# Four-layer hybrid trunk in fp32 on one core: the first block pairs built together, and the dense layers' matrix products kept in source order

## Chip, cores and metric

One core of one Trainium2 chip. The metric is the device time of one execution in microseconds; for the kernel before it is the median of three runs. Further readings come from one profiled execution.

## The reference, cut to what matters

```python
def rmsnorm(x, g):
    y = x * lax.rsqrt(jnp.mean(x * x, axis=-1, keepdims=True) + RMS_EPS)
    return y * g

def short_conv_mixer(h, w_in, conv_w, w_out):
    b_gate, c_gate, z = jnp.split(h @ w_in, 3, axis=-1)
    conv = causal_depthwise_conv(c_gate * z, conv_w)      # width 3
    return (b_gate * conv) @ w_out

def swiglu_ffn(h, w_gate, w_up, w_down):
    return (jax.nn.silu(h @ w_gate) * (h @ w_up)) @ w_down

def reference(x, ...):                                    # x: 512 tokens x 1024
    for i in range(4):                                    # conv, gating, retention, conv
        x = x + mixer[i % 3](rmsnorm(x, norm_mix_g[i]))
        x = x + swiglu_ffn(rmsnorm(x, norm_ffn_g[i]))     # hidden width 2816
    return rmsnorm(x, final_norm_g)
```

The gating and the retention mixer are not touched by the change and are left out here. All is float32.

## The kernel before, in words

**Layout.** `x` lies transposed in SBUF, features on partitions: four tiles `x0` to `x3` of 128 x 1024, each a pair of 128-feature blocks by 512 tokens. The RMS norm is not applied to `x` ahead of a layer: products are made with `x` times its gain, and their results are multiplied by the token's scale afterwards (`normed`), so the scale may come late.

**Three products for one.** The products on TensorE (PE) take operands of type `F32R`. Each float32 operand is split into a high part (a cast on ScalarE, ACT) and a low part (source minus high part, on VectorE, DVE) by `split` (L174); a product is then high x high, high x low and low x high into one PSUM accumulator. `product` (L181 to L195) issues these matmuls at L193; of its last term it issues all three at the end, so that a late last operand holds back only those.

**Seven-part form.** In the conv mixers and in the FFNs a pair of 128-column blocks of weights, against pairs of input blocks and two halves of the tokens (256 each, `H`), is multiplied by a scheme with seven products instead of eight (`columns7`, L211). It uses sums of the inputs (`th`, `tl`, made by `operand_sums`, L409 to L429, from `x` times gain) and sums of the weights (L136 to L139 and the split of the sums). Three accumulators, `c1`, `c5` and `c2` (names ending in 1, 5 and 2 in the program), take the seven parts, 12 matmuls of 256 columns each. `c1` is used several times: between its parts ACT or DVE reads it, at L240, L245 and, with a sign flip, L256:

```python
        part(c1, 3, xt, 1, False)
        with self.tc.high_priority(SOON):
            nc.vector.scalar_tensor_tensor(y[:, 2 * H : 3 * H], c1, -1.0, m5, ALU.mult, ALU.subtract)
        def end():
            part(c1, 2, xt, 3, False)
            nc.scalar.mul(y[:, 3 * H :], c1, -1.0)
            self.held.append(partial(then, y))
        self.late = end
```

The last part, `end`, and what follows from the result (`then`) are put off: `finish` (L284) issues them in the next form, behind that form's first two parts. The plain form with eight products, `columns4` (L262), has two accumulators of 512 columns, 24 matmuls each, and calls `finish` at its start. The first block pair of each layer (`m == 0`) uses the plain form, as the input sums are not needed there.

**Layers.** `conv` loops over four block pairs `m`; for each it builds the three projections `pc`, `pz`, `pb`, and DVE and ACT work out the gated convolution (`first`, `second`, `third`, L575 to L595), which leaves the operands `yh`, `yl`. `ffn` loops over eleven block pairs of the hidden width in four parts: `pg`, `pu`, then SiLU and product leave `hidh`, `hidl`; the down projection `out` of a part is issued by `leave` behind the first `pg` of the next part. `leave` (L433 to L464) adds `out` to `x` (L457), and in its final pass makes the next layer's operands (`operand`, L406 and L407, or L403, L420 and the splits) and the squares (L318 to L322). `end` does this for the last layer, in token halves.

**Scale.** In the first `then` of a layer, `scale_in_psum` sums the squares to a column per 128 tokens by small matmuls (L366, named `scale`), ACT takes a root (L333) and DVE four small steps (L334 to L337); a diagonal (L383) and one more matmul (L384, named `rps`) spread the scale over the partitions. `end` does it through `last_scale`.

**What sets the order.** The program is written in source order, and a scheduler then orders each engine's instructions by a model of its own; products may pass each other. `keep_in_program_order` ties an instruction to the one before it on its engine in source order; before the change only the scale's small matmuls (L368) and the last norm's products have it. The mixed layers (gating, retention) run in `mixed()`, the convs and the FFNs in `dense()`; only inside `dense()` is the pool `self.w7` set, and it holds the weights of the seven-part products.

**Weights and the start.** `plan` and `plan7` list the weight chunks in the order of use; `weights` fetches up to three chunks ahead of the one in use, each half chunk through one of four `raw` buffers of 512 KB by a DMA on SyncE's queue (L127 for the plain form), and splits it. At the start, `run` loads `x0` in two halves, then `x1` to `x3` whole (512 KB each); between them `first_weights` (L166) loads the first plain `pc` chunk in four pieces of 256 KB. The `pz` and `pb` chunks of the first pair follow as ordinary chunks of two 512 KB transfers. `begun` is the last operand made of the loaded `x`; the input sums and the squares of the first layer are issued behind it, in the middle of the first round of `conv`'s loop.

Of the kernel before, what the change touches and what calls it, by code (L numbers as in the profile page):

```python
# [17 lines left out]
P = 128  # L18
# [24 lines left out]
class Kernel:  # L43
# [72 lines left out]
    def prepare7(self, i):  # L116


        nc = self.nc
        src, _, plain = self.chunks[i]  # L120
        out = [[] for _ in range(8)]
        for half in range(2):
            if plain:
                raw = self.raw.tile([P, 4, NB // 4, P], F32, tag="raw", name=f"raw{i}{half}")
                h, l = (self.wp.tile([P, 4, NB // 4, P], F32R, tag=part, name=f"w{part}{i}{half}") for part in "hl")
                if i:
                    nc.sync.dma_start(raw, src[half])  # L127
                    self.split(raw, h, l)
                else:
                    self.first.append((raw, src[half], h, l))  # L130
                for j in range(4):
                    out[j] += [(h[:, j, k], l[:, j, k]) for k in range(NB // 4)]
                continue
            raw = self.raw.tile([P, 4, NB // 4, P], F32, tag="raw", name=f"raw{i}{half}")
            sums = self.sums.tile([P, 4, NB // 4, P], F32, tag="sums", name=f"sums{i}{half}")
            nc.sync.dma_start(raw, src[half])  # L136
            nc.vector.tensor_add(sums[:, :2], raw[:, 3:].broadcast_to([P, 2, NB // 4, P]), raw[:, :3:2])  # L137
            nc.vector.tensor_add(sums[:, 2], sums[:, 1], raw[:, 0])
            nc.vector.tensor_add(sums[:, 3], sums[:, 2], raw[:, 1])  # L139
            for x, n, first, pool in ((raw, 3, 0, self.w7), (sums, 4, 3, self.wp)):  # L140
                h, l = (pool.tile([P, n, NB // 4, P], F32R, tag=part, name=f"w{part}{i}{half}{n}") for part in "hl")
                self.split(x[:, :n], h, l)
# [20 lines left out]
        self.next += 1  # L163
        return self.ready.pop(i)

    def first_weights(self, i, j):  # L166

        raw, src, h, l = (t[:, j : j + 2] for t in self.first[i])
        self.nc.sync.dma_start(raw, src)
        self.split(raw, h, l)  # L170

    def split(self, src, h, l):

# [8 lines left out]
    def product(self, ps, terms, first=True, last=True, more=False):  # L182
# [7 lines left out]
        lh, ll, rh, rl = terms[-1]  # L190
        seq += [(lh, rh), (lh, rl), (ll, rh)]
        for i, (x, y) in enumerate(seq):
            nc.tensor.matmul(  # L193
                ps, x, y, start=first and i == 0, stop=last and i == len(seq) - 1, skip_group_check=more
            )  # L195

    def columns(self, name, acts):

# [66 lines left out]
    def columns4(self, name, then, hold=False, kept=True):  # L265
# [6 lines left out]
        for even, odd in ((0, 1), (3, 2)):  # L272
# [3 lines left out]
                terms += [(*w[even][k], h[:, :T], l[:, :T]), (*w[odd][k], h[:, T:], l[:, T:])]  # L276
            self.product(ps, terms)
            out.append(ps)
        y = self.hid.tile([P, 2 * T], F32, tag="hid", name=name + "y") if kept else self.temp(name + "y")
        for b in range(2):  # L280
            nc.scalar.copy(y[:, b * T : (b + 1) * T], out[b])
        self.held.append(partial(then, y))

    def finish(self, hold=False):  # L284

# [277 lines left out]
        else:  # L563
            self.leave(hid, g, seven)

    def conv(self, j, g, seven, start=False):
        nc = self.nc
        self.r = None
        cw = self.conv_w
# [28 lines left out]
            self.split(y, h, l)  # L598
            acts.extend([(h[:, :T], l[:, :T]), (h[:, T:], l[:, T:])])

        for m in range(NB // 2):
            form = self.columns7 if m else self.columns4
            form("pc", first)
            if m == 3:
# [1 line left out]
            if start and m == 2:  # L606
                form = partial(self.columns4, kept=False)
            form("pz", partial(second, m), m == 0)
            if start and m == 0:
                with self.tc.issue_after(self.begun.ins):  # L610
                    for k in range(NB // 2):
                        self.operand_sums(k, 0)
                    for k in range(NB // 2):
                        self.squares(self.x[k])
            form = self.columns7 if m else self.columns4
            form("pb", third, start and m == 0)
        before = acts[2:]
        begun = [self.begin("out", before) for _ in range(BEGUN)]
        self.finish()
# [217 lines left out]
    def run(self):  # L837
        nc, a = self.nc, self.a
        for i in range(DEPTH):
            j, kind = divmod(i, 3)  # L840
            if kind == 0:
                for m in range(NB // 2):
                    for part in (1, 2, 0):
                        self.plan7(a["conv_w_in"][j, part * NB // 2 + m], m == 0 or (i, m, part) == (0, 2, 2))
                        if m == 3 and part == 1:
# [47 lines left out]
        for _ in range(WARM):  # L893
            nc.tensor.matmul(warm, self.mean_d, self.mean_d, start=True, stop=True)
        nc.scalar.copy(self.const.tile([P, 1], F32, name="first"), self.mean_d[:, :1])
        self.first = []
        self.ready[0] = self.prepare(0)
        for k in range(half):
            if k:
                nc.sync.dma_start(  # L900
                    self.x[k].rearrange("p (b t) -> p b t", b=2),
                    a["x"][2 * k * P : 2 * (k + 1) * P, :].rearrange("(b p) t -> p b t", b=2),
                )
                self.operand(2 * k, 0)
                self.begun = self.operand(2 * k + 1, 0)
                self.first_weights(*((1, 0), (0, 2), (1, 2))[k - 1])
            else:
                for b in range(2):
                    nc.sync.dma_start(self.x[0][:, b * T : (b + 1) * T], a["x"][b * P : (b + 1) * P, :])
                    self.operand(b, 0)  # L910
                    if b == 0:
                        self.first_weights(0, 0)
        nc.sync.dma_start(self.conv_w, a["conv_w"])
        with self.dense():
            self.conv(0, 1, True, True)
            self.ffn(0, 2, False)
        with self.mixed():
            self.sgu(0, 3, True)
# [93 lines left out]
```

## Time and profile before

| | before |
| --- | --- |
| time, median of 3 runs | 2432.98 us (2431.72 to 2434.72) |
| the profiled execution's own time | 2432.58 us |
| its span in the trace | 2430.7 us |
| mean granted clock of PE, share of full speed | 0.997 |
| busy: PE / weight load / DVE / ACT | 2413.3 / 2166.7 / 1807.2 / 1131.8 us |
| mean DMA rate over the span | 100 GB/s |

The span runs from the first to the last instruction of the profile; the time of an execution is 1.9 us longer here. Busy time is the sum of an engine's instructions; PE is TensorE, DVE is VectorE, ACT is ScalarE, SP is SyncE, whose queue carries most DMAs. In a row, `pc<-xh,wh` means that the instruction writes `pc` from `xh` and `wh` (buffer numbers left out), and `L193` is the line of the kernel before. "Idle before" is the time in which the engine waited ahead of the instruction, with the instruction that ended the wait behind the arrow.

### The profile page before, as it was taken

How to read it: one execution, taken by the hardware profiler on the slowest of the kernel's cores; microseconds unless marked ns; L12 is line 12 of the kernel's file. 1: busy time of each engine (PE TensorE's matmuls, PEld its weight loads, DVE VectorE, ACT ScalarE, POOL GpSimd, SP SyncE). 2: the span in 40 equal slices, each digit the busy share in tenths (PEclk: the TensorE clock that was granted, in tenths of full speed). 3: DMA queues.
4: the chain of work that ended last, by engine and by line, in shares of the span. 5: the costliest groups of instructions: out<-in, count | busy, mean ns of one | idle time of the engine just before them, and what ended most of it. 6: DMA issues, size and time to landing. Idle time of an engine off the chain costs nothing.

```text
span 2430.7 us, 36335 instructions
## 1 busy us (share of the span) xinstructions
PE 2413.3 (99%) x14668; PEld 2166.7 (89%) x14668; DVE 1807.2 (74%) x2617; ACT 1131.8 (47%) x1628; POOL 53.0 (2%) x58
## 2 busy tenths in 40 slices
PE   9999999999999999999999999999999999999998
PEld 8988999988888899999888888899999898899998
DVE  8978978863757888777565464888777897978875
ACT  6545445443324544445433333545445654545444
POOL 0000000000101000000000000000000000000000
PEclk9999999999999999999999999999999999999999
DMA  4232333233333233233222232223233223233231
GB/s 157 93 125 61 118 109 103 88 117 119 96 105 95 74 111 120 87 105 122 91 74 87 74 111 76 95 96 114 91 109 105 87 79 135 73 113 104 91 119 53
DMA packets 79129, 242.02 MB, mean 100 GB/s; under 512 B 8816, under 2 KB 12912, under 8 KB 78960
## 3 DMA queue, kind: packets, MB, share of 16 engines
q1 hardware_dynamic: 77728, 238.61, 30.6%
q8 instruction: 115, 1.88, 0.3%
q10 hardware_dynamic: 1232, 1.09, 0.1%
q14 instruction: 54, 0.44, 0.1%
HBM read 237.56 MB, written 2.10 MB: 99 GB/s over the span
## 4 chain that ended last, share of the span: by engine, by line
PE 96%; DVE 3%; ACT 1%; issue 0%; DMA 0%; SPq 0%; DVEq 0%; ACTq 0%
PE out L193 28%; PE pu L193 22%; PE pg L193 22%; PE pv L193 7%; PE pb L193 3%; PE pc L193 3%; PE pz L193 3%; PE q L193 2%; PE k L193 2%; PE po L193 1%; DVE wl L174 1%; PE ps L697 1%; PE ps L193 1%; DVE x L457 0%; PE rps L384 0%
## 5 line engine op out<-in xcount | busy, mean ns | idle before, releaser
L174 ACT CAST wh<-raw 128x768 fp32r<-128x768 f32 (+3 forms) x502 | 429.2, 861 | 623.8 <-PE out L193 197.3
L174 DVE TENSOR_TENSOR wl<-raw,wh 128x768 fp32r<-128x768 f32 (+3 forms) x502 | 488.5, 985 | 150.4 <-ACT wh L174 147.2
L193 PE MATMUL out<-hidl,wh 128*128 128x512 f32 (+1 forms) x736 | 278.3, 381 | 0.0
L174 ACT CAST wh<-sums 128x1024 fp32r<-128x1024 f32 x194 | 201.1, 1050 | 163.9 <-DVE sums L139 77.9
L193 PE MATMUL out<-hidh,wh 128*128 128x512 f32 (+1 forms) x736 | 274.7, 381 | 0.0
L174 DVE TENSOR_TENSOR wl<-sums,wh 128x1024 fp32r<-128x1024 f32 x194 | 233.7, 1219 | 16.6 <-ACT wh L174 9.2
L193 PE MATMUL out<-hidh,wl 128*128 128x512 f32 (+1 forms) x736 | 204.9, 380 | 0.0
L193 PE MATMUL pg<-xh,wh 128*128 128x256 f32 (+1 forms) x672 | 202.4, 318 | 1.3 <-ACT xh L174 1.3
L193 PE MATMUL pu<-xh,wh 128*128 128x256 f32 (+1 forms) x672 | 200.9, 316 | 0.0
L193 PE MATMUL pg<-xl,wh 128*128 128x256 f32 (+1 forms) x672 | 200.7, 315 | 0.0
L193 PE MATMUL pu<-xl,wh 128*128 128x256 f32 (+1 forms) x672 | 200.1, 314 | 0.0
L457 DVE TENSOR_TENSOR x<-out,x 128x512 f32<-128x512 f32 x192 | 130.5, 685 | 81.2 <-PE out L193 80.9
L193 PE MATMUL pg<-th,wh 128*128 128x256 f32 x640 | 168.6, 284 | 2.5 <-ACT wh L174 2.5
L193 PE MATMUL pg<-tl,wh 128*128 128x256 f32 x640 | 168.7, 284 | 0.0
L193 PE MATMUL pu<-tl,wh 128*128 128x256 f32 x640 | 168.0, 283 | 0.0
L193 PE MATMUL pu<-th,wh 128*128 128x256 f32 x640 | 167.9, 283 | 0.0
L193 PEld LDWEIGHTS out<-hidl,wh 128*128 128x128 f32 x736 | 138.6, 188 | 24.8
L193 PEld LDWEIGHTS out<-hidh,wh 128*128 128x128 f32 x736 | 137.9, 188 | 24.5
L193 PEld LDWEIGHTS out<-hidh,wl 128*128 128x128 f32 x736 | 136.0, 188 | 26.2
L193 PE MATMUL pu<-xh,wl 128*128 128x256 f32 (+1 forms) x672 | 153.2, 313 | 0.0
L193 PE MATMUL pg<-xh,wl 128*128 128x256 f32 (+1 forms) x672 | 149.5, 313 | 0.0
L137 DVE TENSOR_TENSOR sums<-raw 128x512 f32<-128x512 f32 x194 | 130.2, 685 | 15.5 <-DMA raw<-in_ffn_w_up 13.4
(270 smaller groups left out, 5533.6 us busy)
## 6 DMA issues: line engine op xcount, KB each, us to landing
raw<-in_ffn_w_gate SPq DMA_DIRECT2D x88, 512.0 KB, 3.5
raw<-in_ffn_w_up SPq DMA_DIRECT2D x88, 512.0 KB, 3.6
raw<-in_ffn_w_down SPq DMA_DIRECT2D x96, 384.0 KB, 3.3
raw<-in_conv_w_in SPq DMA_DIRECT2D x46, 512.0 KB, 3.9
raw<-in_sgu_w_v SPq DMA_DIRECT2D x16, 512.0 KB, 3.5
raw<-in_sgu_w_u SPq DMA_DIRECT2D x16, 512.0 KB, 3.5
raw<-in_sgu_w_out SPq DMA_DIRECT2D x16, 512.0 KB, 3.5
raw<-in_ret_w_qk SPq DMA_DIRECT2D x16, 512.0 KB, 3.5
```

The source lines that it names most:

```text
L137: nc.vector.tensor_add(sums[:, :2], raw[:, 3:].broadcast_to([P, 2, NB // 4, P]), raw[:, :3:2])
L174: return self.nc.scalar.copy(h, src), self.nc.vector.tensor_sub(l, src, h.bitcast(F32))
L193: nc.tensor.matmul(ps, x, y, start=first and i == 0, stop=last and i == len(seq) - 1, skip_group_check=more)
L457: nc.vector.tensor_add(x[:, s], ps, x[:, s])
L697: nc.tensor.matmul(ps[:, c * P : (c + 1) * P], v[m // 4][c][:, col], ws[grp // 4][:, at], start=True, stop=True)
```

## The change

It has two parts.

1. **First block pairs together.** `begin_all` builds the first block pair of the three projections of the first conv in one loop over the four pairs of input blocks `k`: for each it loads the two halves of `x[k]` (256 KB each) and a piece of 256 KB of each projection's weights, makes the operands and splits the pieces, and issues the products into six accumulators (two per projection). `conv` gets these accumulators as `start`, copies them out with `blocks_out` (the former end of `columns4`), then issues the input sums and squares, and its loop starts at `m = 1`. The plan of the first layer starts at `m = 1` as well. `first_weights` goes.
2. **Order kept.** In `product`, each matmul issued while `self.w7` is set is tied to the instruction ahead of it on PE by `keep_in_program_order`. That holds for all products of the convs and FFNs, and not for the mixed layers or `begin_all`, which runs ahead of `dense()`.

```diff
-    def first_weights(self, i, j):
-        raw, src, h, l = (t[:, j : j + 2] for t in self.first[i])
-        self.nc.sync.dma_start(raw, src)
-        self.split(raw, h, l)
+    def begin_all(self, srcs):
+        nc = self.nc
+        out = [[self.acc("first") for _ in range(2)] for _ in srcs]
+        parts = []
+        for k in range(NB // 2):
+            half, at = divmod(k, NB // 4)
+            if at == 0:
+                parts = [
+                    [self.wp.tile([P, 4, NB // 4, P], F32R, tag=part, name=f"w{part}f{k}") for part in "hl"]
+                    for _ in srcs
+                ]
+            xs = []
+            for n, src in enumerate(srcs):
+                raw = self.raw.tile([P, 4, P], F32, tag="raw", name=f"rawf{k}{n}")
+                h, l = (t[:, :, at] for t in parts[n])
+                if n == 0:
+                    for b in range(2):
+                        m = 2 * k + b
+                        nc.sync.dma_start(self.x[k][:, b * T : (b + 1) * T], self.a["x"][m * P : (m + 1) * P, :])
+                        self.begun = self.operand(m, 0)
+                        if b == 0:
+                            nc.sync.dma_start(raw, src[half][:, :, at])
+                            self.split(raw, h, l)
+                else:
+                    nc.sync.dma_start(raw, src[half][:, :, at])
+                    self.split(raw, h, l)
+                xh, xl = self.xs[k]
+                for ps, blocks in zip(out[n], ((0, 1), (3, 2))):
+                    terms = [
+                        (h[:, j], l[:, j], xh[:, b * T : (b + 1) * T], xl[:, b * T : (b + 1) * T])
+                        for b, j in enumerate(blocks)
+                    ]
+                    self.product(ps, terms, k == 0, k == NB // 2 - 1)
+        return out
...
-            nc.tensor.matmul(
+            mm = nc.tensor.matmul(
                 ps, x, y, start=first and i == 0, stop=last and i == len(seq) - 1, skip_group_check=more
             )
+            if self.w7:
+                self.tc.keep_in_program_order(mm)
...
-        for m in range(NB // 2):
+        if start:
+            for name, out, then in zip(("pc", "pz", "pb"), start, (first, partial(second, 0), third)):
+                self.blocks_out(name, out, then)
+            with self.tc.issue_after(self.begun.ins):
+                for k in range(NB // 2):
+                    self.operand_sums(k, 0)
+                for k in range(NB // 2):
+                    self.squares(self.x[k])
+        for m in range(1 if start else 0, NB // 2):
...
-                for m in range(NB // 2):
+                for m in range(0 if i else 1, NB // 2):
...
+        first = self.begin_all([a["conv_w_in"][0, part * NB // 2] for part in (1, 2, 0)])
         nc.sync.dma_start(self.conv_w, a["conv_w"])
         with self.dense():
-            self.conv(0, 1, True, True)
+            self.conv(0, 1, True, first)
```

Line numbers shift: L174 becomes L209, L193 becomes L228, L240, L245, L256 and L260 become L280, L282, L293 and L297, L366 becomes L400, L383 and L384 become L417 and L418.

**The order on PE, at three places.** Numbers behind names are buffer numbers; `x4` is a run of equal rows.

The first is the scale of the first conv, on PE, in the kernel before: around its small matmuls stand products of the second block pair (`pc5` is `c5` of `pc`, `pc1` its `c1`).

```order
L193 MATMUL pc5_469<-xl2_139,wh314_383 128x256
L193 MATMUL pc5_469<-xh0_117,wl304_370 128x256
L193 MATMUL pc5_469<-xh1_128,wl304_370 128x256
L366 MATMUL scale_501<-mean_d_94,sum_348 128x1 x4
L193 MATMUL pc5_469<-xh2_138,wl314_384 128x256
L193 MATMUL pc5_469<-xh3_148,wh314_383 128x256
```

and further down, behind `pz`, its `rps`:

```order
L193 MATMUL pz5_614<-xh3_148,wh414_464 128x256
L193 MATMUL pz5_614<-xl3_149,wh414_464 128x256
L384 MATMUL rps_514<-rs_513,mean_d_94 128x512
L193 MATMUL pz5_614<-xh3_148,wl414_465 128x256
L193 MATMUL pc1_468<-th0_311,wh303_365 128x256
L193 MATMUL pc1_468<-tl0_312,wh303_365 128x256
```

Now, on PE at the same place:

```order
L228 MATMUL pc5_490<-tl3_419,wh014_457 128x256
L228 MATMUL pc5_490<-th3_418,wl014_458 128x256
L400 MATMUL scale_522<-mean_d_94,sum_422 128x1 x4
L418 MATMUL rps_535<-rs_534,mean_d_94 128x512
L228 MATMUL pc1_489<-th0_385,wh004_443 128x256
L228 MATMUL pc1_489<-tl0_386,wh004_443 128x256
```

Thirty-nine rows stood between the scale's matmuls and `rps`; now there are none, and the products behind stand behind both.

The second is the first FFN, on PE, at a last part of a `pg` in the seven-part form (`pg1` is its `c1`); before, where a part of it (weights `wh32..4`, `wl32..4`) ends and the down projection follows:

```order
L193 MATMUL pg1_2401<-th2_1903,wl3214_2279 128x256
L193 MATMUL pg1_2401<-th3_1963,wh3214_2278 128x256
L193 MATMUL pg1_2401<-tl3_1964,wh3214_2278 128x256
L193 MATMUL pg1_2401<-th3_1963,wl3214_2279 128x256
L193 MATMUL out_2523<-hidl_2447,wh33_2385 128x512
L193 MATMUL out_2523<-hidh_2196,wl33_2386 128x512 x2
L193 MATMUL out_2523<-hidh_2446,wl33_2386 128x512
L193 MATMUL out_2523<-hidh_2446,wh33_2385 128x512
```

Now, at the same product (weights `wh29..4`, then `wh29..3`):

```order
L228 MATMUL pg1_2422<-th2_1924,wl2914_2300 128x256
L228 MATMUL pg1_2422<-th3_1984,wh2914_2299 128x256
L228 MATMUL pg1_2422<-tl3_1985,wh2914_2299 128x256
L228 MATMUL pg1_2422<-th3_1984,wl2914_2300 128x256
L228 MATMUL pg1_2422<-th0_1813,wh2903_2281 128x256
L228 MATMUL pg1_2422<-tl0_1814,wh2903_2281 128x256
L228 MATMUL pg1_2422<-th1_1846,wh2903_2281 128x256
L228 MATMUL pg1_2422<-tl1_1847,wh2903_2281 128x256
```

Before, `out` stands between the part of `c1` that the sign flip reads and the part that `end` adds (`wh3203`, 21 rows below the last of `wl3214`'s); now `end`'s part (`wh2903`) follows directly.

The third is the end of the first conv, on PE (`pb1` is `c1` of the last `pb`). Before:

```order
L193 MATMUL pb1_1565<-tl3_345,wh1913_1454 128x256
L193 MATMUL pb1_1565<-th3_344,wl1913_1455 128x256
L193 MATMUL out_1832<-yh_904,wh24_1693 128x512
L193 MATMUL out_1832<-yl_905,wh24_1693 128x512
L193 MATMUL out_1832<-yh_904,wh24_1693 128x512
L193 MATMUL out_1832<-yl_905,wh24_1693 128x512
L193 MATMUL out_1832<-yh_1241,wh24_1693 128x512
L193 MATMUL out_1832<-yl_1242,wh24_1693 128x512
```

Now:

```order
L228 MATMUL pb1_1586<-tl3_419,wh1613_1475 128x256
L228 MATMUL pb1_1586<-th3_418,wl1613_1476 128x256
L228 MATMUL out_1692<-yh_1782,wh17_1570 128x512
L228 MATMUL out_1692<-yl_1783,wh17_1570 128x512
L228 MATMUL out_1692<-yh_1782,wl17_1571 128x512
L228 MATMUL out_1692<-yh_1782,wh17_1570 128x512
```

The operands `yh_1782`, `yl_1783` come from this `pb`; before, `out` products with operands of earlier pairs stand behind `pb`'s last matmul, and now those with the last pair's operands.

## Rows read from the trace of the kernel before

**Rows 1.** The page, part 1: busy time, share of the span, instructions of each engine.
```profile
PE 2413.3 (99%) x14668; PEld 2166.7 (89%) x14668; DVE 1807.2 (74%) x2617; ACT 1131.8 (47%) x1628; POOL 53.0 (2%) x58
```

**Rows 2.** Windows: us, busy (x instructions) by engine, PE's clock, DMA share, GB/s.
```profile
5.00:11.50 6.50, 4.61 (x13) 2.07 (x12) 4.92 (x8) 4.80 (x9) 0.00 (x0) 1.00 1.01 362
11.50:42.40 30.90, 30.90 (x137) 25.57 (x138) 29.07 (x44) 25.14 (x34) 0.00 (x0) 1.00 0.54 173
128.00:131.00 3.00, 1.59 (x13) 1.39 (x13) 3.00 (x6) 1.32 (x2) 0.00 (x0) 1.00 0.42 131
189.50:193.00 3.50, 1.61 (x8) 0.91 (x6) 2.60 (x5) 3.50 (x6) 0.00 (x0) 1.00 0.66 200
193.00:198.00 5.00, 4.99 (x17) 4.09 (x18) 4.81 (x7) 5.00 (x8) 0.00 (x0) 0.66 0.00 0
2078.00:2083.00 5.00, 5.00 (x18) 4.12 (x19) 4.82 (x7) 5.00 (x8) 0.00 (x0) 0.68 0.00 0
2421.50:2424.50 3.00, 1.24 (x3) 0.50 (x2) 1.07 (x5) 0.17 (x1) 0.00 (x0) 0.67 0.26 87
```

**Rows 3.** Chain of waits, 0 to 60 us: start us, us, what.
```profile
20.68 10.88 PE pz L193 x48
...
42.44 3.95 PE pc L193 x33
...
53.47 0.79 PE scale L366 x8
...
59.03 0.86 PE rps L384 x2
```

**Rows 4.** Timeline of PE from 5 us: start us, us, engine, line, operation.
```profile
5.61 0.62 PE L193 MATMUL pc<-xh,wh 128*128 128x512 f32 x1
```

**Rows 5.** Timeline of DVE, 44 to 50.5 us.
```profile
44.99 1.22 DVE L174 TENSOR_TENSOR tl<-xt,th 128x1024 fp32r<-128x1024 f32 x1
...
49.07 0.68 DVE L327 SCALAR_TENSOR_TENSOR sum<-sum 128x512 f32<-128x512 f32 x1
```

**Rows 6.** Timeline of all engines, 2421 to 2425 us; in brackets idle before and releaser.
```profile
2421.59 0.17 ACT L333 ACTIVATE rtok<-scale 128x2 f32<-128x2 f32 x1 [0.52 <-PE scale L366]
...
2422.71 0.43 DVE L383 TENSOR_TENSOR diag<-eye,rtok 128x256 f32<-128x256 f32 x1
...
2423.28 1.19 PE L384 MATMUL rps<-diag,mean_d 128*128 128x256 f32 x2 [1.74 <-DVE diag L383]
```

**Rows 7.** Groups by shape on DVE, 0 to 58 us: busy us, mean ns, idle before.
```profile
L383 DVE TENSOR_TENSOR rs<-eye,rtok 128x512 f32<-128x512 f32 x1 | 0.7, 691 | 0.1
...
L256 DVE SCALAR_TENSOR_TENSOR pcy<-pc,pcm 128x256 f32<-128x256 f32 x1 | 0.4, 425 | 0.0
```

**Rows 8.** Timeline of ACT, 52 to 55 us.
```profile
52.94 1.28 ACT L333 ACT_TABLE_LOAD   x1
```

**Rows 9.** Timeline of all engines, 157.6 to 165.7 us.
```profile
159.75 0.28 PE L193 MATMUL pb<-th,wl 128*128 128x256 f32 x1
...
160.69 0.38 ACT L260 ACTIVATE pby<-pb 128x256 f32<-128x256 f32 x1
...
164.04 1.23 DVE L174 TENSOR_TENSOR yl<-pby,yh 128x1024 fp32r<-128x1024 f32 x1 [1.11 <-ACT yh L174]
...
165.56 0.40 PE L193 MATMUL out<-yl,wh 128*128 128x512 f32 x1
```

**Rows 10.** Timeline of all engines, 1551 to 1562.5 us.
```profile
1552.10 0.39 PE L193 MATMUL pg<-xh,wh 128*128 128x512 f32 x1
...
1560.06 1.29 DVE L174 TENSOR_TENSOR xl<-xg,xh 128x512 fp32r<-128x512 f32 x2
```

**Rows 11.** Timeline of all engines, 808 to 817 us.
```profile
809.07 0.39 PE L193 MATMUL pg<-xh,wh 128*128 128x512 f32 x1
...
815.55 0.69 DVE L174 TENSOR_TENSOR xl<-xg,xh 128x512 fp32r<-128x512 f32 x1
```

**Rows 12.** Timeline of PE, 189 to 193.8 us.
```profile
191.55 0.38 PE L193 MATMUL pg<-th,wh 128*128 128x256 f32 x1 [1.26 <-ACT wh L174]
```

More of the change, by code (lines that the diff above doesn't have):

```diff
@@ L125, in prepare7 @@
                 h, l = (self.wp.tile([P, 4, NB // 4, P], F32R, tag=part, name=f"w{part}{i}{half}") for part in "hl")
-                if i:
-                    nc.sync.dma_start(raw, src[half])
-                    self.split(raw, h, l)
-                else:
-                    self.first.append((raw, src[half], h, l))
+                nc.sync.dma_start(raw, src[half])
+                self.split(raw, h, l)
                 for j in range(4):
@@ L164, in weights, with blocks_out @@
         return self.ready.pop(i)
-    def first_weights(self, i, j):
-        raw, src, h, l = (t[:, j : j + 2] for t in self.first[i])
-        self.nc.sync.dma_start(raw, src)
-        self.split(raw, h, l)
+    def begin_all(self, srcs):
[23 more added lines that the diff above has]
+                    nc.sync.dma_start(raw, src[half][:, :, at])
+                    self.split(raw, h, l)
+                xh, xl = self.xs[k]
[6 more added lines that the diff above has]
+        return out
+    def blocks_out(self, name, out, then, kept=True):
+        y = self.hid.tile([P, 2 * T], F32, tag="hid", name=name + "y") if kept else self.temp(name + "y")
+        for b in range(2):
+            self.nc.scalar.copy(y[:, b * T : (b + 1) * T], out[b])
+        self.held.append(partial(then, y))
     def split(self, src, h, l):
@@ L278, in columns4 @@
             out.append(ps)
[L279 to L282, printed above, removed]
+        self.blocks_out(name, out, then, kept)
     def finish(self, hold=False):
@@ L564, in ffn, with conv @@
             self.leave(hid, g, seven)
-    def conv(self, j, g, seven, start=False):
+    def conv(self, j, g, seven, start=()):
         nc = self.nc
@@ L608, in conv @@
             form("pz", partial(second, m), m == 0)
[L609 to L614, printed above, removed]
             form = self.columns7 if m else self.columns4
-            form("pb", third, start and m == 0)
+            form("pb", third)
         before = acts[2:]
@@ L895, in run @@
         nc.scalar.copy(self.const.tile([P, 1], F32, name="first"), self.mean_d[:, :1])
[L896 to L912, printed above, removed]
+        first = self.begin_all([a["conv_w_in"][0, part * NB // 2] for part in (1, 2, 0)])
         nc.sync.dma_start(self.conv_w, a["conv_w"])
         with self.dense():
-            self.conv(0, 1, True, True)
+            self.conv(0, 1, True, first)
             self.ffn(0, 2, False)
```

## Prediction

> **What bounds the kernel now.** The first part of the page comes first: TensorE (PE) is busy 2413.3 of 2430.7 us, VectorE (DVE) 1807.2 [rows 1]. PE's queue sets the end, so a wait put into it lengthens the run and a wait taken out shortens it. The windows say where PE is not busy [rows 2]: 1.9 of 6.5 us while x and the first weights land, 1.4 of 3.0 from 128 on, 1.9 of 3.5 from 189.5 on. After that last one, 5 us run at a granted clock of 0.66, a mix of its two levels; the same happens at 2078. In the chain of waits the reader is to see the pitch of the matmuls [rows 3]: 48 of 512 columns take 10.88 us, 0.227 each; 33 of 256 columns 3.95 us, 0.12 each. Elsewhere PE runs at this pitch: a scheduler has set its order, and wherever one product's input is late, another product stands in front of it. All idle time that could be won is about 4.2 (start) + 1.4 + 2 x 1.9, and 2 x 1.7 for the clock, since 5 us at 0.66 lose 34%: 12.8 us.
>
> **The change, part by part.** Both programs hold 14,518 matmul instructions, so PE's own work stays. Moved are the order of the first block and, in every stage with seven-part products, the freedom of matmuls to pass each other.
>
> *First block and first scale.* The first product starts at 5.61 [rows 4] and the third projection ends at 42.44 [rows 3]; 144 products at 0.227 are 32.6, so 4.2 us are waits for loads. Now each pair of x feeds 36 products (8.2 us) and needs five transfers of 256 KB, 1.31 MB, at 362 GB/s [rows 2] 3.6 us. SyncE issues seven transfers more, hidden behind this; ScalarE (ACT) and DVE have four casts and four differences more, smaller ones, of the same elements. The block should end near 38.5. That gain is then spent: the next two parts of `pc` take 1.4 and 1.1 us, to 41.1, and then the product with the last `tl` must come, and behind it the scale, which needs the last sum of squares. DVE had these at 46.2 and 49.75 [rows 5]. It was busy 29.07 of the 30.9 us ahead [rows 2] and has the same work before them now, so they cannot come much sooner; up to 2.8 us later is possible, since the next weights wait for one of four raw buffers, which now turn over in smaller pieces. So: scale from 49.8 to 52.5, 0.8 for it [rows 3], 2.0 for the chain behind it (next part), 0.86 for `rps`: done at 53.5 to 56.2, mean 54.9. The kernel before had as much work behind it at 42.44 + 2.88 + 0.79 + 0.86 = 47.0. **Loss 7.9**, bounds 4 and 11.
>
> *Scale to rps, six more places* (four FFNs, second convolution, end). In source order `rps` follows `scale` directly. Between them lie a root on ACT and five instructions on DVE. At the end of the kernel that was already so [rows 6]: `rps` starts at 2423.28 after 1.74 idle, so the scale was over at 2421.54. With the wider diagonal, 691 against 430 ns [rows 6, 7], it is 2.0. Before, 4.8 us between them were filled with other products (53.47 + 0.79 to 59.03, [rows 3]). Three FFNs 2.0 each; the FFN behind the gating layer needs a table load of 1.28 [rows 8], of which 0.7 is not covered by the scale's own products, 2.7; in the convolution the load stands behind a copy and three sums stand between the small steps, 3.9; end 1.7. **Sum 14.3**; bounds 10.4 (six times 1.7) and 20 (DVE in the middle of another instruction each time).
>
> *Sign flip, 19 places.* In a seven-part product DVE reads `c1` with a sign flip at L256, and `end()` then adds its last part into the same `c1`. Normally the next form's two parts stand between. Where a plain form, a `leave` or the end of a group follows, nothing does: I count 19 runs of 24 matmuls into one `c1` in the new order, none before. The trace has no such wait. Built from rows: 0.28 for the last matmul [rows 9], 0.05 to the reader (2421.54 to 2421.59, [rows 6]), 0.425 for the instruction [rows 7], 0.14 back to PE (2422.71 + 0.43 to 2423.28, [rows 6]), less one pitch of 0.12: 0.775, taken as 0.77. **Sum 14.6.** Bounds: the instruction alone, 8; twice the price, if DVE is caught in a longer instruction, 28. I take the sum, as its order of DVE puts little directly ahead of L256.
>
> *End of the convolution, twice.* `pb`'s last matmul starts at 159.75 and ends its pitch at 159.87 [rows 9]; ACT first does two casts, and its flip starts at 160.69; DVE multiplies, ACT casts, and `yl` is over at 164.04 + 1.23 = 165.27. Before, products of two later columns filled this: 22 of 0.227 stand between 159.87 and 165.56, so 0.7 was idle. Now `out` needs `yh` in its first and `yl` in its second matmul: 165.27 + 0.14 - 159.87 - 0.23 = 5.3 idle. **Sum 2 x 4.6 = 9.2**; without the 0.8 for which the flip waits 7.6; at most 10.5.
>
> *Layer boundaries.* The plain `pg` needs the first half of the last x after 13 of 24 matmuls, 2.95 us, the second half after 22.5. Behind the retention layer `pg` starts at 1552.10, needs the first `xl` of the last pair at 1555.05 and gets it at 1560.06 + 0.69 = 1560.75 [rows 10]: 5.7, as DVE's order there is the same in both programs. Behind the gating layer only the last half is late: `pg` starts at 809.07, needs it at 814.2, and it is there at 815.55 + 0.69 = 816.24 [rows 11]: 2.0. Behind the third FFN (into the second convolution) I work out 0.8 from the new DVE order at the same durations. Behind the two convolutions it comes to 4.5 and 5.2 in the same way, where the kernel before lost 1.9 each [rows 2]: 2.6 and 3.3. **Sum 14.4**; bounds 6 and 20.
>
> *Ends of the FFNs.* The last `out` needs the low part of the last hidden block after nine matmuls (2.04 us). The chain from flip to difference takes 160.69 to 165.27 [rows 9], 4.6; with its three wide instructions at 0.69 [rows 7] instead of 1.23 it is 2.9. So 0.9 three times, and 1.8 at the end, where the matmuls are half as long. **Sum 4.5**; 0 to 8. Against this, the 1.4 us at 128 should go, since DVE is ahead there.
>
> *Clock.* The clock fell after the 3.5 us with 1.9 idle, and not after the one idle stretch of 128 to 131 [rows 2]. Waits of 4 us and more are new in five places (first block, two convolution ends, retention boundary, second convolution's scale): 5 x 1.7 = **8.5**; bounds 0 and 20. The Trainium skill, "TensorE: Matmul & The Clock Gate", section "HAM oscillation — how this bites in real kernels", describes loops in which the clock falls again at every wait between groups of matmuls. By that rule the clock term would be that of the third rival below; the trace agrees only in part, as the wait at 128 was not followed by a fall.
>
> **Sum.** 7.9 + 14.3 + 14.6 + 9.2 + 14.4 + 4.5 - 1.4 + 8.5 = 72.0 us. The profiled execution took 2432.58 (span 2430.7 and 1.9 around it), 0.4 under the median: 2432.6 + 72.0 = **2505**, rounded.
>
> **The rivals.**
> *It gets faster.* Mechanism: with PE in source order, DVE and ACT prepare operands in that same order, and no product waits behind another's late input; at the two convolution-to-FFN boundaries the kernel before waits for exactly such preparations, a cast of weights by ACT [rows 12]. It decides if the new waits stay under the 12.8 us that can be won; if all of these are won, 2420. Against it: seven scale chains of at least 1.7 are 12 us already, and their order is fixed. Chance 0.03.
> *Only the fixed chains cost.* What is late at boundaries is prepared earlier, because PE's other waits let DVE run ahead: start gain -4.2, scale chains 14.3 + 2.0, flips 14.6, and half of the convolution ends, 4.6: 31 us, 2464. For it: DVE idles a quarter of the time [rows 1]. Against: at boundaries the late thing starts from PE's last product. Chance 0.2.
> *The clock falls behind every scale chain and boundary too.* Some 17 places instead of 5: 12 x 1.7 = 20 us on top, 2525. For it: the stretch 2421.5 to 2424.5 runs at 0.67 [rows 2], and holds just a scale chain. Against: 128 to 131. Chance 0.15.
> *It does not matter.* If the late inputs were as late as PE, gains and losses would cancel: chance 0.02; the orders show that the change does what it says.
>
> **Numbers.** Forecast 0.6. The range takes in all of it, most of the second rival and the third: 2462 to 2540. A measurement of this kernel can tell 0.2%, 5 us. Slower by more 0.94, within 0.03, faster 0.03.
>
> **What would show it.** In the profile after: PE's waits name DVE's diagonal some 1.7 to 2.0 us in each of six or seven places, in all 12 to 17 us; PE waits for L293 about 0.7 us 19 times; `out` waits for `yl` or `yh` about 5 us twice; `pg` waits for `xl` after the retention layer; PE idle in 5 to 12 shrinks below 1 us but 6 us and more stand between 40 and 56; the mean clock falls from 0.997. Wrong would be: PE busy at the old pitch behind `scale`, or a span under 2450.

## The result, and the profile after

| | before | after |
| --- | --- | --- |
| time, median | 2433.24 us (4 runs, 2431.72 to 2434.72) | 2532.59 us (4 runs, 2530.97 to 2534.85) |
| ratio to before | | 1.0409, 95% interval 1.0391 to 1.0427 |
| the profiled execution / its span | 2432.58 / 2430.7 us | 2530.97 / 2529.2 us |
| mean granted clock | 0.997 | 0.984 |

The change makes the kernel slower by 99 us. Of the executions reported below, one of `pin_inside`'s ten took 3996.64 us at a mean clock of 0.555; it counts in that median, which would be 2438.19 us without it, and not in the ratio. From the page of after, part 1:

```profile
PE 2443.0 (97%) x14668; PEld 2185.5 (86%) x14668; DVE 1829.7 (72%) x2621; ACT 1147.7 (45%) x1632; POOL 51.9 (2%) x58
```

PE is busy 30 us longer with the same 14,668 instructions, and the span is 98.5 us longer [rows 1]: some 68 us are new idle time, and most of the rest is the same work at a lower clock. The mean clock does not say where it fell, so that has to be looked for stretch by stretch.

What PE waits for in after (its waits by instruction and releaser; the columns are us in total, times, longest):

```profile
PE rps L418 <- DVE rs L417: 15.8, 6, 4.7
PE pg L228 <- DVE xl L209: 9.9, 7, 3.6
PE pg L228 <- ACT xh L209: 8.2, 3, 3.8
PE out L228 <- ACT yh L209: 8.1, 2, 4.0
PE pg L228 <- DVE pgy L293: 7.1, 12, 0.8
PE rps L418 <- DVE diag L417: 5.3, 2, 3.5
PE scale L400 <- DVE sum L361: 5.0, 1, 5.0
PE out L228 <- DVE hidl L209: 3.7, 5, 0.9
PE pc L228 <- DVE pcy L293: 3.2, 3, 1.8
PE pz L228 <- DVE wl L209: 2.4, 2, 1.6
PE pu L228 <- DVE puy L293: 2.4, 4, 0.6
PE pc L228 <- DVE tl L209: 1.8, 1, 1.8
PE out L228 <- DVE yl L209: 1.5, 3, 0.8
PE pc L228 <- DVE xl L209: 1.5, 1, 1.5
PE pc L228 <- ACT th L209: 1.3, 1, 1.3
```

Four groups are to be seen. `rps` waits for its diagonal 6 + 2 times, 21.1 us. `pg` and `pu`, with `pc`, wait for `pgy`, `puy`, `pcy`, the sign flip of L293: 12 + 4 + 3 = 19 times, 12.7 us. `pg`, `pc` and `out` wait for operands at the layer boundaries and ends (`xl`, `xh`, `yh`, `yl`, `hidl`). And the first convolution waits for `sum`, `tl`, `th`. Before, of these only short waits at the start, near 129 us and at two boundaries were there, and the last diagonal's [rows 2, 6, 12].

Windows of after, at the start and at the first scale (us, busy by engine, clock, DMA share, GB/s):

```profile
5.00:11.50 6.50, 6.33 (x27) 5.04 (x26) 5.16 (x8) 4.89 (x8) 0.00 (x0) 1.00 1.09 334
11.50:42.40 30.90, 30.23 (x144) 25.27 (x142) 27.80 (x45) 25.77 (x39) 0.00 (x0) 1.00 0.59 183
42.40:57.00 14.60, 5.24 (x15) 3.65 (x16) 11.77 (x20) 6.15 (x9) 0.00 (x0) 0.56 0.23 73
```

The first two answer to [rows 2]: PE is busy 6.33 of 6.5 us where it was 4.61, so the start is won. From 42.4 on it is lost again: 5.24 us of work in 14.6, at a clock of 0.56 (half speed is the lower level, 1.2 GHz), while DVE works 11.77.

One of the 19 waits for the flip, and the first of the two scale chains in `end`, from timelines of after (in brackets the idle time ahead and its releaser):

```profile
267.23 0.39 PE L228 MATMUL pg<-th,wh 128*128 128x256 f32 x1 [0.81 <-DVE pgy L293]
```

```profile
2503.78 1.28 ACT L367 ACT_TABLE_LOAD   x1
...
2506.13 0.42 DVE L417 TENSOR_TENSOR diag<-eye,rtok 128x256 f32<-128x256 f32 x1
...
2506.70 1.19 PE L418 MATMUL rps<-diag,mean_d 128*128 128x256 f32 x2 [3.52 <-DVE diag L417]
```

Adding up windows of 2 us over the whole span gives PE 85.0 us idle against 16.6 before; and PE's busy time, each window weighted with the share of the clock that it was not granted, comes to 28.3 us against 3.8. So in this execution the clock costs **24.5 us** of the 98.5, and the waits about 68; some 5 us of longer busy time are left over, and what they are is not shown. (The profiled execution is the fastest of the four; the others have a mean clock of 0.983.) In after the clock drops in 14 stretches, each behind a wait of PE, and in the last scale at the end, which is as before.

### The profile page after: what moved, and what is told of

It is laid out like the page before. It is cut to its first block, busy times and chain, and to the rows that moved or that the text cites. A ratio compares the mean times of both kernels' runs of the same rounds, so it can differ in the third digit from the quotient of the medians.

```text
span 2529.2 us, 36410 instructions
## 1 busy us (share of the span) xinstructions
PE 2443.0 (97%) x14668; PEld 2185.5 (86%) x14668; DVE 1829.7 (72%) x2621; ACT 1147.7 (45%) x1632; POOL 51.9 (2%) x58
## 5 line engine op out<-in xcount | busy, mean ns | idle before, releaser
L209 ACT CAST wh<-raw 128x768 fp32r<-128x768 f32 (+3 forms) x494 | 423.1, 862 | 541.4 <-PE out L228 208.8
L209 DVE TENSOR_TENSOR wl<-raw,wh 128x768 fp32r<-128x768 f32 (+3 forms) x494 | 481.7, 988 | 144.1 <-ACT wh L209 142.3
L209 ACT CAST wh<-sums 128x1024 fp32r<-128x1024 f32 x194 | 198.4, 1050 | 244.2 <-PE out L228 103.6
L228 PE MATMUL out<-hidl,wh 128*128 128x512 f32 (+1 forms) x736 | 280.4, 383 | 3.9 <-DVE hidl L209 3.7
L228 PE MATMUL out<-hidh,wh 128*128 128x512 f32 (+1 forms) x736 | 279.9, 382 | 0.5 <-ACT hidh L209 0.5
L209 DVE TENSOR_TENSOR wl<-sums,wh 128x1024 fp32r<-128x1024 f32 x194 | 232.3, 1220 | 51.7 <-PE pu L228 20.5
L228 PE MATMUL pg<-xl,wh 128*128 128x256 f32 (+1 forms) x672 | 204.3, 319 | 9.9 <-DVE xl L209 9.9
L228 PE MATMUL pg<-xh,wh 128*128 128x256 f32 (+1 forms) x672 | 204.2, 319 | 8.2 <-ACT xh L209 8.2
L228 PE MATMUL out<-hidh,wl 128*128 128x512 f32 (+1 forms) x736 | 205.0, 381 | 0.0
L228 PE MATMUL pu<-xh,wh 128*128 128x256 f32 (+1 forms) x672 | 200.8, 314 | 0.0
L228 PE MATMUL pu<-xl,wh 128*128 128x256 f32 (+1 forms) x672 | 200.2, 313 | 0.0
L228 PE MATMUL pg<-th,wh 128*128 128x256 f32 x640 | 172.5, 291 | 7.1 <-DVE pgy L293 7.1
L228 PE MATMUL pu<-th,wh 128*128 128x256 f32 x640 | 167.7, 284 | 2.4 <-DVE puy L293 2.4
L228 PE MATMUL pg<-tl,wh 128*128 128x256 f32 x640 | 169.3, 286 | 0.0
L228 PEld LDWEIGHTS out<-hidl,wh 128*128 128x128 f32 x736 | 139.4, 189 | 32.6 <-DVE hidl L209 6.9
L228 PE MATMUL pu<-tl,wh 128*128 128x256 f32 x640 | 167.3, 283 | 0.0
L228 PEld LDWEIGHTS out<-hidh,wh 128*128 128x128 f32 x736 | 139.5, 190 | 26.6 <-ACT hidh L209 0.7
L228 PEld LDWEIGHTS out<-hidh,wl 128*128 128x128 f32 x736 | 136.9, 189 | 26.0
L228 PE MATMUL pg<-xh,wl 128*128 128x256 f32 (+1 forms) x672 | 152.5, 321 | 0.0
L228 PEld LDWEIGHTS pg<-xl,wh 128*128 128x128 f32 x672 | 130.2, 194 | 20.7 <-DVE xl L209 13.1
L228 PE MATMUL pu<-xh,wl 128*128 128x256 f32 (+1 forms) x672 | 148.0, 313 | 0.0
```

Source lines behind the costliest of these rows:

```text
L209: return self.nc.scalar.copy(h, src), self.nc.vector.tensor_sub(l, src, h.bitcast(F32))
L228: mm = nc.tensor.matmul(ps, x, y, start=first and i == 0, stop=last and i == len(seq) - 1, skip_group_check=more)
```

## The experiments

Each ran beside the kernel before on the same chip; ratios are to that. Beside them the kernel before took 2431.58 to 2433.24 us (medians), so a difference of 2 us between two of these times says nothing. The theory: products in source order stand still wherever they meet a chain of other engines, and the clock falls behind these waits; the new first block costs next to nothing. The main rivals: the first block is what costs; order costs everywhere; the clock falls for other reasons.

### One half of the change at a time

`begin_only` is the changed kernel without the tie:

```diff
-            if self.w7:
-                self.tc.keep_in_program_order(mm)
```

> The changed kernel without the tie on the products; the first block pairs stay together. Theory (the kept order costs, the new first block is nearly free): products pass each other again, so the waits for the diagonal, for the sign flip and for the operands at layer boundaries go: 2427 to 2440 us, no PE wait for the diagonal but at the kernel's end, mean clock 0.995 or more. Rival (the new first block is a good part of the loss, through later sums of squares and smaller weight transfers): 2445 us or more, with the lost time before 60 us.

Measured: 2427.77 us, ratio 0.9982 (0.9973 to 0.9992). Its windows at the start, and all that PE waits for above 1.0 us in sum, the warm-up left out:

```profile
5.00:11.50 6.50, 6.35 (x28) 4.64 (x27) 4.72 (x8) 4.32 (x8) 0.00 (x0) 1.00 0.97 302
11.50:42.40 30.90, 30.90 (x152) 26.20 (x151) 26.96 (x42) 24.78 (x37) 0.00 (x0) 1.00 0.61 184
42.00:60.00 18.00, 17.48 (x146) 17.28 (x146) 16.95 (x31) 12.61 (x19) 0.00 (x0) 1.00 0.20 60
```

```profile
PE rps L416 <- DVE diag L415: 1.7, 1, 1.7
PE pg L228 <- ACT wh L209: 1.6, 2, 0.8
PE pg L228 <- ACT xh L209: 1.3, 2, 0.6
```

The new first block alone makes the kernel **faster** by 0.18% and beats both kernels. It wins the start: the columns of the first 144 products are through at 38.5 us, where the kernel before needs 42.1. It also has one fall of the clock fewer, that of 193 to 198 us [rows 2]. What was lost from 42.4 on in the tied order is not lost here: PE works 17.48 of 18 us, because products of `pz` and `pb` stand where it waited for `sum` and `tl`.

`pin_only` is the kernel before with the tie added in `product`.

> The kernel before with the tie on the products alone; its first block as it was. Theory: 2522 to 2540 us, 19 PE waits for the sign flip, 12 to 14 us, and the clock falling at the same layer boundaries and scales as in the changed kernel. Rival (the new first block costs 20 us or more): below 2512 us.

Measured: 2533.54 us, ratio 1.0415 (1.0399 to 1.0430), as the whole change. From its waits of PE (L193 is `product` in it):

```profile
PE pg L193 <- DVE pgy L258: 7.1, 12, 0.8
...
PE pc L193 <- DVE pcy L258: 4.2, 3, 2.7
...
PE pu L193 <- DVE puy L258: 2.4, 4, 0.6
PE scale L368 <- DVE sum L329: 2.2, 1, 2.2
```

The flips wait 19 times here too. At the first scale PE waits 2.2 us for `sum` instead of 5.0, since it arrives later: the start's gain of the new first block is a longer wait behind it when the order is kept. Behind the first scale `pin_only` has done the same work at 64.4 us, after at 65.7. The two halves do not add: -4.4 us alone, nothing on top of the tie. That the two times agree to 1 us is in part chance: `pin_only`'s trace has 4.7 us less idle time than after's and 7.2 us more loss by the clock (35.5). A part of that is a fall from 9 to 16 us, inside the old first block, which the trace of the kernel before does not have.

### Where order costs

`pin_inside` ties products only in the inner part of the FFNs (`self.inside` is set for `m >= 2` in `ffn`'s loop and cleared ahead of its last `finish`), `pin_edges` only elsewhere:

```diff
-            if self.w7:
+            if self.w7 and self.inside:
                 self.tc.keep_in_program_order(mm)
```

> The products tied only inside the FFNs, from the third block pair to the last, without the last down projection; free in the convolutions, at layer boundaries and at the scales. Theory (source order costs only where it meets a chain of other engines): 13 waits for the sign flip at some 0.6 us, 8 us over the untied kernel's 2427.8: 2433 to 2439 us, no more falls of the clock than the untied one has. Rival (order costs everywhere, for example through weights that come late): 2445 us or more.

Measured: 2438.39 us, ratio 1.0023 (1.0013 to 1.0032).

```profile
PE pg L229 <- DVE pgy L294: 7.9, 13, 1.3
```

The 13 flips are there, 7.9 us, and beside them one more flip of 0.5 is all that is much above what the untied kernel waits for. PE is busy 2410.3 us, the untied kernel's 2410.6: the tie as such takes no time. In the profiled execution the mean clock is 0.999, and it did not fall behind any of the flips.

> The complement: products tied in the convolutions, in the first two block pairs of each FFN and in its last down projection, free in between. Theory: nearly the whole loss, 2532.6 less about 8: 2520 to 2528 us. Rival (loss spread over all products): below 2500 us.

Measured: 2529.38 us, ratio 1.0397 (1.0380 to 1.0415), 1.4 us above what was expected, and nearly the whole loss. The two kernels' losses against the untied one, 10.6 and 101.6 us, sum to 112 where the full tie costs 105: an edge tied alone waits a little more (8.8 us for `hidl` in place of 3.7), and the clock's loss in its trace is 33.1 us against 28.3. Source order costs at convolutions, boundaries, scales and group ends; in the long middle of the FFNs, which holds most products, it costs its flips only.

### The scale chain

`scale_early` writes the scale's matmuls one product form ahead of the spreading matmul:

```diff
+        tok, self.tok = self.tok, None
+        if tok is None:
+            tok = self.scale_of_tokens(self.squares_done())
...
+                if m == 0:
+                    self.tok = self.scale_of_tokens(self.squares_done())
```

> The changed kernel with the scale's small matmuls written 24 products (FFNs) or 48 products (second convolution) ahead of the matmul that spreads the scale, in five of the seven places. Theory: the five waits for the diagonal, 2.04 + 3.01 + 2.12 + 4.70 + 2.05 = 13.9 us, go, and with them five falls of the clock at about 1.7 us each, 8.5: 2507 to 2513 us. Rival A (the clock falls for another reason than these waits): 2516 to 2521 us with the falls still there. Rival B (the scale now waits for the sums of squares instead): 2525 us or more, with PE waits for sum ahead of the scale.

Measured: 2516.31 us, ratio 1.0346 (1.0331 to 1.0362): 16.3 us better than the change, where 22 were expected. The time lies in rival A's range, but rival A's sign is not there: behind none of the five scales does the clock fall. The theory held in part. Of the waits for `rs` the longest, 4.70, went; the four in the FFNs shrank to 1.3 to 1.7 us each, so that all of them fell from 15.8 to 7.6 us:

```profile
PE rps L419 <- DVE rs L418: 7.6, 5, 1.9
```

DVE's timeline at the first FFN's scale shows why:

```profile
235.62 1.22 DVE L210 TENSOR_TENSOR wl<-sums,wh 128x1024 fp32r<-128x1024 f32 x1
...
237.09 0.17 DVE L369 RECIPROCAL rtok<-rtok 128x4 f32<-128x4 f32 x1
237.18 0.66 DVE L135 TENSOR_TENSOR sums<-raw 128x512 f32<-128x512 f32 x1
237.76 0.15 DVE L370 TENSOR_TENSOR rt<-rtok 128x4 f32<-128x4 f32 x1
237.87 0.43 DVE L136 TENSOR_TENSOR sums<-sums,raw 128x256 f32<-128x256 f32 x1
...
238.86 0.69 DVE L418 TENSOR_TENSOR rs<-eye,rtok 128x512 f32<-128x512 f32 x1
```

Between the small steps L369 to L372, of some 0.15 us, stand sums of weights of 0.66 and 0.42 us, and ahead of the first a split of 1.22. A chain that starts early is queued into DVE's other work: from the reciprocal, 237.09, to the end of the diagonal, 239.55, it takes 2.5 us; in after the same steps took 1.7 (236.08 to 237.82). So of the gain 8.2 us are waits for `rs`; the clock's loss, added up as above, fell by 8.6, from 28.3 to 19.7 us.

`begin_early` is the same cure in the untied kernel, as a control.

> The untied kernel (first block pairs together, no product tied) with the scale written early as in scale_early. Theory: where products may pass each other no wait for the diagonal was left but at the end, so the cure that gave 16 us in the tied order gives nothing: 2425 to 2430 us, as the untied kernel's 2427.8. Rival (an earlier scale helps in itself): below 2424 us.

Measured: 2428.20 us, ratio 0.9982 (0.9973 to 0.9992): no change against 2427.77, as expected. There was no wait to cure.

`scale_untied` ties each product to the product before it only:

```diff
-            if self.w7:
-                self.tc.keep_in_program_order(mm)
+            with self.tc.issue_after(self.last_mm.ins) if self.w7 and self.last_mm else nullcontext():
+                mm = nc.tensor.matmul(
...
+            if self.w7:
+                self.last_mm = mm
```

> The changed kernel with each product tied to the product before it, and no longer to the scale's matmuls and to the spreading one between them. Theory: the scheduler puts products between scale and spreading again; the waits of 1.93, 2.04, 3.01, 2.12, 4.70, 2.05 and 3.52 us go, 19.4, and with them six falls at 1.7: 2500 to 2510 us. Rival (the same waits come back as waits of other products behind): 2520 us or more.

Measured: 2495.40 us, ratio 1.0261 (1.0246 to 1.0276), 37 us better than the change, more than the 29 expected. No wait for `rs` is left, and the 5.0 us for `sum` are gone too. One wait came back elsewhere: a flip in the first convolution, at 90.5 us,

```profile
90.53 0.58 PE L230 MATMUL pc<-th,wh 128*128 128x256 f32 x1 [5.75 <-DVE pcy L295]
```

which was 1.8 us in after (at 95.1). Idle time fell by 23.2 us and the clock's loss from 28.3 to 16.4.

### The sign flip

`flip_cover` exchanges two parts in `columns7`, so that 12 matmuls into `c5` stand between the flip and the last part of `c1`:

```diff
-        part(c5, 6, xs, 2, False)
-        add(y[:, :H], c5, u2)
         part(c1, 3, xt, 1, False)
         with self.tc.high_priority(SOON):
             nc.vector.scalar_tensor_tensor(y[:, 2 * H : 3 * H], c1, -1.0, m5, ALU.mult, ALU.subtract)
+        part(c5, 6, xs, 2, False)
+        add(y[:, :H], c5, u2)
```

> The changed kernel with two parts of the seven-part form exchanged in the source, so that a part into c5 stands between the sign flip of c1 and the last part into c1. Theory: the 19 waits for the sign flip, 12.7 us in all, fall under 2 us, and little else moves: 2517 to 2524 us. Rival (another wait on c1 takes their place, since the copy that empties c1 now has one part instead of two to hide behind): 2527 to 2537 us, with PE waiting for ACT's copy.

Measured: 2529.71 us, ratio 1.0394 (1.0377 to 1.0412): 2.9 us less than the change instead of 12. The time lies in the rival's range, and the two intervals overlap, so a gain is not shown. From its waits of PE (flips are L291 here):

```profile
PE out L228 <- DVE hidl L209: 8.1, 4, 2.3
...
PE pg L228 <- ACT pgm L286: 3.9, 4, 1.1
...
PE pc L228 <- DVE pcy L291: 1.1, 1, 1.1
```

The flips fell from 12.7 to 1.1 us, so the mechanism is as told; but the gain was spent: PE's idle time is 85.3 us by the page, 86.2 in after. `hidl` waits 8.1 us in place of 3.7, since the quarter of the result that comes from `c5` is ready 12 matmuls later and the end of each FFN needs it; ACT's copy `pgm` is waited for, 3.9, as the rival had it; and `wl` and `xh` are waited for some 1 us more each. The clock's loss, 32.2 us against 28.3, is no proof of a further cost: `pin_only`, `pin_edges` and `first_late`, whose flips are as they were, have 32.8 to 35.5.

### The clock

`fill_wait` gives PE something to do in the scale's wait, eight products whose result is overwritten:

```diff
+        if fill:
+            h = self.xs[0][0]
+            for _ in range(8):
+                self.tc.keep_in_program_order(self.nc.tensor.matmul(ps, h[:, :P], h[:, :T], start=True, stop=True))
         self.nc.tensor.matmul(ps, self.mean_d, t, start=True, stop=True)
```

> The changed kernel with eight more products of 512 columns, 1.8 us of work whose results are thrown away, put between the scale's small matmuls and the matmul that spreads the scale, in the four FFNs. They fill most of waits of 2.0, 3.0, 2.1 and 2.1 us and take no time from what follows. Theory (the clock falls because PE stands still there): the four falls behind them go and with each some 1.7 us, 6.8 in all: 2523 to 2528 us. Rival (the falls have another cause): still there, 2531 to 2536 us.

Measured: 2526.82 us, ratio 1.0389 (1.0373 to 1.0404), 5.8 us better than the change with more work on PE, as the theory had it. The windows of 6 us behind the four scales and behind one boundary (the second row of each), in after:

```profile
237.00:243.00 6.00, 5.12 (x25) 4.63 (x26) 2.23 (x4) 2.59 (x3) 0.00 (x0) 0.72 0.01 3
848.00:854.00 6.00, 5.46 (x17) 4.36 (x18) 3.23 (x6) 2.41 (x3) 0.00 (x0) 0.72 0.55 175
873.00:879.00 6.00, 5.08 (x24) 4.04 (x25) 1.99 (x3) 1.66 (x2) 0.00 (x0) 0.72 0.00 0
1634.00:1640.00 6.00, 6.00 (x36) 5.75 (x35) 2.90 (x4) 2.60 (x3) 0.00 (x0) 0.72 0.00 0
2184.00:2190.00 6.00, 6.00 (x37) 5.76 (x36) 2.96 (x4) 2.60 (x3) 0.00 (x0) 0.72 0.00 0
```

and in `fill_wait`:

```profile
236.00:242.00 6.00, 5.90 (x37) 4.75 (x36) 3.19 (x8) 1.30 (x2) 0.00 (x0) 1.00 0.01 3
846.00:852.00 6.00, 4.43 (x19) 3.68 (x20) 4.26 (x8) 2.41 (x3) 0.00 (x0) 1.00 0.65 190
870.00:876.00 6.00, 4.93 (x36) 4.21 (x35) 2.25 (x5) 2.21 (x2) 0.00 (x0) 1.00 0.00 0
1630.00:1636.00 6.00, 5.99 (x44) 5.51 (x45) 2.36 (x3) 2.64 (x4) 0.00 (x0) 1.00 0.00 0
2178.00:2184.00 6.00, 5.90 (x36) 4.74 (x36) 3.01 (x8) 1.46 (x3) 0.00 (x0) 1.00 0.00 0
```

Behind each scale the clock was 0.72 over 6 us, a loss of 1.7, and is 1.00 now. By themselves these windows do not show that the filling did it. At the boundary no product was added, PE waits 2.09 us for `xl` as it did in after (2.08), and yet the clock did not fall this time. And `flip_cover`, which fills nothing, has the same wait at the first FFN's scale and no fall behind it:

```profile
238.27 1.13 PE L418 MATMUL rps<-rs,mean_d 128*128 128x512 f32 x2 [2.04 <-DVE rs L417]
```

```profile
237.00:243.00 6.00, 3.99 (x26) 3.31 (x26) 2.26 (x5) 2.26 (x3) 0.00 (x0) 1.00 0.01 3
```

In the five traces in which these waits are left whole (after, `pin_only`, `pin_edges`, `flip_cover`, `first_late`), the clock fell behind 6 of the 15 scale waits of 2.0 to 2.1 us, and behind all five of 3.01 us in the second FFN. So a wait of about 2 us may be followed by a fall and may not, in the same place.

What speaks for the filling is the time: each of its four executions is shorter than each of the change's four, with a mean clock of 0.985 to 0.986 against 0.983 to 0.984. In its trace the clock's loss is 23.8 us against 28.3, with one new fall elsewhere, near 1960 us. By the ratios the gain is 4.9 us, and their intervals overlap a little. So it is likely, for the four waits taken together, that PE's standing still brings the falls; for a single one it is not shown.

### The first scale

`first_late` puts the first convolution's scale one form later, `form("pc", first, bool(start) and m == 1)`, so that more products stand ahead of it.

> The changed kernel with the first convolution's scale written one form later (behind the first two parts of the second pz instead of the second pc), order still kept. Theory (PE meets the sums of squares too early: it stands 5.04 us for the sum and 1.93 for the diagonal, and works at half the clock around them): four parts more, 5.4 us, stand ahead of the scale; the 5.04 falls under 1 us, the low clock from 45 to 57 us gives back some 3 us of the 5.9 that PE worked in it: 2523 to 2528 us. Rival (DVE is late for everything there, so PE waits as long for tl and wl instead): 2529 to 2535 us.

Measured: 2531.55 us, ratio 1.0404 (1.0389 to 1.0420), no gain; the time lies in the rival's range. PE no longer waits for `sum`, but for others of DVE's and ACT's results in turn:

```profile
44.85 0.58 PE L228 MATMUL pc<-th,wh 128*128 128x256 f32 x1 [1.61 <-ACT th L209]
47.05 0.58 PE L228 MATMUL pc<-tl,wh 128*128 128x256 f32 x1 [1.62 <-DVE tl L209]
...
64.60 2.07 PE L418 MATMUL rps<-rs,mean_d 128*128 128x512 f32 x2 [4.17 <-DVE rs L417]
```

(1.25, 1.81 and 1.93 us in after.) DVE is busy 17.22 of the 18 us from 42 to 60 here, and by 78.4 us PE has done the work that it had done by 78.2 in after: in whichever order it meets DVE's results, it loses about as much. `begin_only` shows what helps, other products that need none of these results, and these the kept order holds back.

## Why the prediction was right, and where it was not

The forecast was slower, 2505 in a range of 2462 to 2540; 2532.59 lies in the range, 28 us above the likeliest value and closer to the third rival's 2525. Term by term, in us against the kernel before; measured are sums of the waits in the trace of after, less what the kernel before waited there; the clock's row is the sum over windows told above:

| term | predicted | measured |
| --- | --- | --- |
| first block and first scale | 7.9 | 9.0 (1.25 + 1.81 + 5.04 + 1.93, less 1.0 won before 42.4) |
| scale to `rps`, six more places | 14.3 | 17.4 (2.04, 3.01, 2.12, 4.70, 2.05, 3.52) |
| sign flip, 19 places | 14.6 | 12.7 |
| end of the convolution, twice | 9.2 | 9.0 (4.04 + 0.46 + 4.04 + 0.76, less 0.3) |
| layer boundaries | 14.4 | 15.8 (9.9 + 8.2 + 1.5 less 3.8) |
| ends of the FFNs | 4.5 | 4.2 |
| the place at 128 | -1.4 | +1.0 (1.57 against 1.41, and 0.86 new in the second convolution) |
| clock | 8.5 | 24.5 |
| sum | 72.0 | 93.6 of the span's 98.5 |

The waits were right to a few us in all: 63.5 predicted, 69.1 found. They account for all of the new idle time, 68.8 us by the pages. The remaining 4.9 us lie in PE's busy time, which grew by 29.7, and the clock's share in it is 24.5; what the rest is stays open.

**The step that was mis-sized** is the clock: "Waits of 4 us and more are new in five places: 5 x 1.7 = 8.5". It rested on one place of the trace of before, 128 to 131 [rows 2], where 1.4 us idle were not followed by a fall, and read from it that only long waits count. The trace of after shows falls behind the scale chains of 2.0 to 2.1 us as well, and `fill_wait` that with these waits filled the clock costs less. The price of one was right: 0.72 over 6 us is 1.7. The number was not: 14 stretches, some of them long, where PE met several waits in a row (42.4 to 57, 176 to 185). That is nearly the third rival, to which I gave 0.15 and which had 17 places and 28.5 us. Where the count lands is in part luck, since the same waits of some 2 us are followed by a fall in one trace and not in another; in the other kernels with nearly the whole tie (`pin_only`, `pin_edges`, `flip_cover`, `first_late`) the clock's loss is 32.2 to 35.5 us, 4 to 7 more than here. The Trainium skill's section "HAM oscillation — how this bites in real kernels" ("TensorE: Matmul & The Clock Gate"), cited in the prediction for that rival, describes a loop whose clock falls again at every wait between groups of matmuls; its waits are for loads, of some 3 to 5 us. The traces agree for the waits of 3.01 us, with a fall behind all five, and only in part for those of 2.0 to 2.1, with 6 of 15.

**Smaller misses.** The prediction's 14,518 matmuls stand in no trace; both traces have 14,668, so that PE's work stays holds. The chain in `end` was taken at 1.7 from the kernel's last one [rows 6]; the first of the two also waits for a table load of 1.28 that ACT makes there, and took 3.52. The second convolution's was 4.70 against 3.9. The place at 128 got no better: a `wl` that `pz` needs is late there in the new order as well.

**The new first block** did what was worked out: its products are through at 38.5 us in `begin_only` and 38.8 in after, where the prediction had 38.5; its gain exists (4.4 us in `begin_only`), and in the kept order the wait for `sum`, 5.04 us, takes it back (`pin_only` is as slow as both together). Of the rivals, "only the fixed chains cost" falls: the boundaries cost 15.8.

## What to carry to other kernels

An order kept by hand is priced at the few places where it meets a chain through other engines: look for each matmul that reads, or overwrites, what a chain started by the matmul just ahead of it delivers; in the long runs between, it costs little (10.6 us for the inner FFNs, 101.6 for the rest). Add some 1.7 us for the work at the lower clock behind each wait of 3 us and more, and for waits of about 2 us expect it at some of them (6 of 15 here); do not count on one to be spared because another was. Measure the halves of a change apart: here one was worth 4 us and was buried under the other's 100.

## What was not expected

A cover moved in one place uncovers another: `flip_cover` removed 11.6 us of one kind of wait and gained 2.9, which is not clear of noise. An earlier start of a chain does not end it as much earlier, since DVE takes its steps in turn with other work (2.5 us instead of 1.7 in `scale_early`). And the clock's fall behind one and the same wait of 2.1 us came in one run and not in another, so the windows of one trace before and after a cure do not show that the cure worked.
